# Moving rows of the big products begin 32 bytes, not 48 bytes, past a 256-byte line

## The chip, the cores and the metric

The kernel runs on one NeuronCore of one Trainium2 chip. The metric is the device time of that core in microseconds (us). The kernel before took 823.48 us (median of three runs, 822.98 to 824.05). Five engines work side by side: TensorE (PE, with its weight loads listed apart as PEld), VectorE (DVE), ScalarE (ACT), GpSimd (POOL) and SyncE (SP), which only issues transfers here. SBUF is the on-chip memory, seen as 128 partitions; an "address" below is a byte offset within each partition. Matrix products go to PSUM, read only by ACT and DVE.

## The reference

Two layers act on x, 256 tokens by 1024 features, in float32:

```
x = x + 0.5 * swiglu(rms_norm(x, ffn1_norm), ffn1_wi, ffn1_wo)         # wi 1024 x 2816, wo 1408 x 1024
u = rms_norm(x, mix_norm);  c = u @ w_in + b_in                        # w_in 1024 x 6312
y_sb  = stick-breaking attention      (4 heads of 64)
y_ml  = mLSTM, chunks of 128          (4 heads of 128)
y_mla = latent attention with rotary  (4 heads)
g = sigmoid(c.gates)                                                   # three times 1024
x = x + (g0 * (y_sb @ w_up_sb) + g1 * (y_ml @ w_up_ml) + g2 * (y_mla @ w_up_mla)) @ w_out
x = x + 0.5 * swiglu(rms_norm(x, ffn2_norm), ffn2_wi, ffn2_wo)
```

Nearly all of the arithmetic is in the products with `ffn*_wi`, `ffn*_wo`, `w_in`, `w_up_*` and `w_out`: these are the "big products".

## The kernel before, in words

**Three matmuls for one.** Both factors of a big product are split into a high and a low part of type fp32r (`hi`, `lo`), and `mm3` (L604) makes hi·hi, hi·lo and lo·hi, three matmuls that add into one PSUM tile. A matmul has a stationary operand (128 x 128, brought in by its own weight load) and a moving operand whose columns stream past it. In almost all of the big products the weights are stationary and the activations move: 256 columns, one for each token, so each partition reads a contiguous row of 256 x 4 = 1024 bytes. These are `feat_units` (L727: `ffn*_wi` and most of `w_in`), `plan_down` (L800: `ffn*_wo`, `w_out`) and `up_units` (L1086). In a smaller class the activations are stationary and the weights move, in rows of 512, 424 or 256 columns: `tok_units` (L712), the first columns of `w_in` (`first_emit`, L952) and the very last product (`plan_last`, L829).

**Where the weights lie.** SP loads a tile of weights into `raw` (`dma_tile`, L357), ACT casts it to the high part, DVE subtracts to get the low part (`conv_hi`, L364, and `conv_lo`). The two parts go into a ring of five `whi` and five `wlo` tiles, or, in the FFNs and a few other places, into two of eight tiles `g4_0` to `g4_7`. The attention outputs, which are the moving operand of `up_units`, lie in `g4` tiles as well.

**Where the moving rows lie.** `moving` (L250) makes the tiles for the activations: `u` (the normalised x) and `R1` to `R4` (the FFN's hidden activations, and the merged branches). It allocates SHIFT elements more than needed and returns the part behind them. `conv_hi` does the same inside `whi` and `wlo`, when the weights are going to be the moving operand (`w.moves`).

**What sets the addresses.** `Trunk.__init__` allocates all these tags first, in the order of `LAYOUT`. FIRST (16512) is the address at which the first one would begin; ahead of each tag a pad is put in, so that it begins at a multiple of LINE = 256 bytes. The tags' sizes are rounded up to 32 bytes, and a `whi` or `wlo` is 4352 = 17 x 256 bytes, a `g4` 4096 bytes. So every stationary weight tile begins at residue 0 of 256 bytes, and its columns are taken at steps of 512 bytes. A moving row begins at SHIFT x 4 = 48 bytes past such a multiple: rows follow each other at 1024 bytes, so all of them do. There are two exceptions: in `up_units` the moving rows lie in `g4` at residue 0, and so does a moving weight tile that was put into `g4` instead of the ring.

**What sets the order.** One Python program emits all instructions, in an order that it plans by itself: `Flow` (L79) keeps an estimated clock for each engine and for each tile the estimated time at which its pieces are ready; `drive` (L416) goes through the units of the products in order, and slips in conversions (`feed`, L377) and side work where the estimates allow it. The estimates know shapes, types and engines. Addresses come in at one place: `pieces` (L109) divides a tile into pieces of 256 bytes, counted from the tile's own beginning.

Of the kernel before, what the change touches and what calls it, by code (L numbers as in the profile page):

```python
# [202 lines left out]
class Trunk:  # L203
# [2 lines left out]
    SLACK, NEAR, BACK = 0.1, 6, 1.5  # L206


    FIRST, LINE, SHIFT = 16512, 256, 12
    LAYOUT = (("u", 4112, 1), ("R2", 2064, 1), ("R1", 2072, 1), ("R3", 784, 1), ("R4", 784, 1),  # L210
              ("whi", 1088, 5), ("wlo", 1088, 5), *((f"g4_{i}", 1024, 1) for i in range(8)))

# [1316 lines left out]
```

## Time and profile before

| | |
|---|---|
| median of three runs | 823.48 us (822.98 to 824.05) |
| profiled execution, its own time | 823.87 us |
| its span, from the first to the last instruction | 822.1 us |
| PE busy | 814.6 us, 6475 matmuls |
| DVE, ACT, POOL busy | 587.1, 455.4, 35.4 us |
| granted TensorE clock | 1.00 in the mean, the whole span |

A profile shows one execution. Matmuls overlap in the pipeline, so the busy time of one (281 ns or so) is not what it costs: the cost is its pitch, the time from one start to the next, which is read from a run of matmuls that the views put together ("x24" with the run's length). In the names, `mm<-u,whi` is a matmul into a PSUM tile `mm` with moving operand `u` and stationary operand `whi`; numbers of buffers are left out, so `R` is R1 to R4 and `g` is any `g4`.

### The profile page before, as it was taken

How to read it: one execution, taken by the hardware profiler on the slowest of the kernel's cores; microseconds unless marked ns; L12 is line 12 of the kernel's file. 1: busy time of each engine (PE TensorE's matmuls, PEld its weight loads, DVE VectorE, ACT ScalarE, POOL GpSimd, SP SyncE). 2: the span in 40 equal slices, each digit the busy share in tenths (PEclk: the TensorE clock that was granted, in tenths of full speed). 3: DMA queues.
4: the chain of work that ended last, by engine and by line, in shares of the span. 5: the costliest groups of instructions: out<-in, count | busy, mean ns of one | idle time of the engine just before them, and what ended most of it. 6: DMA issues, size and time to landing. Idle time of an engine off the chain costs nothing.

```text
span 822.1 us, 16189 instructions
## 1 busy us (share of the span) xinstructions
PE 814.6 (99%) x6475; PEld 788.0 (96%) x6475; DVE 587.1 (71%) x943; ACT 455.4 (55%) x724; POOL 35.4 (4%) x51
## 2 busy tenths in 40 slices
PE   8999999999999999999999999999999999999998
PEld 6999999899999999999999999998999999999996
DVE  5687878989667488755776567789967585886641
ACT  7456645658675546544554444665576845555430
POOL 0000000200200000000000000110003000000000
PEclk9999999999999999999999999999999999999999
DMA  8678834654264757865576554366543665587611
GB/s 257 197 226 253 266 110 137 202 156 122 85 205 153 233 167 219 258 191 168 155 228 204 179 166 141 105 207 182 157 119 112 200 183 183 179 250 218 185 67 52
DMA packets 122384, 145.41 MB, mean 177 GB/s; under 512 B 7542, under 2 KB 97092, under 8 KB 122308
## 3 DMA queue, kind: packets, MB, share of 16 engines
q1 hardware_dynamic: 122148, 144.30, 57.7%
q8 instruction: 51, 0.84, 0.4%
q14 instruction: 25, 0.20, 0.1%
q10 hardware_dynamic: 160, 0.07, 0.1%
HBM read 143.29 MB, written 1.05 MB: 176 GB/s over the span
## 4 chain that ended last, share of the span: by engine, by line
PE 94%; DMA 2%; ACT 1%; SPq 1%; DVE 1%; issue 0%; POOL 0%; DVEq 0%; ACTq 0%; POOLq 0%
PE mm L189 61%; PE at L189 33%; DMA raw<-in_ffn_wi_dram 2%; SPq L189 1%; ACT g L189 1%; DVE g L189 0%; POOL rstd L189 0%; ACT s2k L189 0%; ACT x L189 0%; ACT whi L189 0%; ACT t L189 0%; DVE s2k L189 0%; ACT u L189 0%; DVE xn L189 0%; DVE t L189 0%
## 5 line engine op out<-in xcount | busy, mean ns | idle before, releaser
L189 PE MATMUL mm<-u,whi 128*128 128x256 f32 x1728 | 312.7, 283 | 0.0
L189 ACT CAST whi<-raw 128x1024 fp32r<-128x1024 f32 (+3 forms) x186 | 190.6, 1032 | 153.9 <-PE mm L189 46.0
L189 PEld LDWEIGHTS mm<-u,whi 128*128 128x128 f32 x1728 | 264.9, 188 | 0.9 <-issue 0.7
L189 DVE TENSOR_TENSOR wlo<-raw,whi 128x1024 fp32r<-128x1024 f32 (+3 forms) x186 | 220.2, 1197 | 57.4 <-ACT whi L189 54.0
L189 PE MATMUL mm<-u,wlo 128*128 128x256 f32 x864 | 242.7, 281 | 0.0
L189 PEld LDWEIGHTS mm<-u,wlo 128*128 128x128 f32 x864 | 162.4, 188 | 0.0
L189 ACT CAST g<-raw 128x1024 fp32r<-128x1024 f32 (+3 forms) x86 | 87.3, 1021 | 79.0 <-PE mm L189 19.7
L189 PE MATMUL mm<-u,g 128*128 128x256 f32 x1056 | 129.3, 281 | 0.7 <-DVE g L189 0.7
L189 PEld LDWEIGHTS mm<-u,g 128*128 128x128 f32 x1056 | 126.6, 188 | 0.9 <-DVE g L189 0.9
L189 DVE TENSOR_TENSOR g<-raw,g 128x1024 fp32r<-128x1024 f32 (+3 forms) x86 | 101.3, 1187 | 28.0 <-ACT g L189 27.5
L189 PE MATMUL at<-R,g 128*128 128x256 f32 x594 | 72.6, 281 | 0.0
L189 PEld LDWEIGHTS at<-R,g 128*128 128x128 f32 x594 | 71.3, 188 | 0.0
L189 PE MATMUL at<-R,whi 128*128 128x256 f32 x388 | 69.5, 281 | 0.0
L189 PEld LDWEIGHTS at<-R,whi 128*128 128x128 f32 x388 | 59.4, 188 | 0.0
L189 PE MATMUL mm<-whi,u 128*128 128x512 f32 (+1 forms) x168 | 56.2, 386 | 0.0
L189 PE MATMUL at<-R,wlo 128*128 128x256 f32 x194 | 54.5, 281 | 0.0
L189 DVE TENSOR_TENSOR R<-s2k,R 128x512 fp32r<-128x512 f32 (+1 forms) x24 | 15.6, 649 | 29.4 <-ACT R L189 29.3
L189 PEld LDWEIGHTS mm<-whi,u 128*128 128x128 f32 x168 | 31.5, 188 | 5.2
L189 PEld LDWEIGHTS at<-R,wlo 128*128 128x128 f32 x194 | 36.5, 188 | 0.0
L189 PE MATMUL mm<-wlo,u 128*128 128x512 f32 (+1 forms) x84 | 32.1, 382 | 0.0
L189 POOL TENSOR_TENSOR rcol<-rcol,mhalf 128x2 f32<-128x2 f32 x6 | 7.0, 1175 | 491.6 <-DVE rcol L189 491.6
L189 ACT ACTIVATE u<-x,cols 128x256 fp32r<-128x256 f32 x40 | 18.2, 501 | 12.6 <-DVE x L189 12.6
(221 smaller groups left out, 995.8 us busy)
## 6 DMA issues: line engine op xcount, KB each, us to landing
raw<-in_w_in_dram SPq DMA_DIRECT2D x92, 512.0 KB
raw<-in_ffn_wi_dram SPq DMA_DIRECT2D x174, 256.0 KB
raw<-in_ffn_wo_dram SPq DMA_DIRECT2D x35, 512.0 KB
raw<-in_w_out_dram SPq DMA_DIRECT2D x16, 512.0 KB
raw<-in_ffn_wo_dram SPq DMA_DIRECT2D x12, 384.0 KB
raw<-in_w_up_ml_dram SPq DMA_DIRECT2D x16, 256.0 KB
raw<-in_w_in_dram SPq DMA_DIRECT2D x8, 424.0 KB
raw<-in_w_up_sb_dram SPq DMA_DIRECT2D x8, 256.0 KB
```

What stands on the lines that cost most here:

```text
L189: f(*args, **kw)
```

## The change

One constant is changed. SHIFT goes from 12 to 8 elements of 4 bytes, and with it the beginning of each moving row made by `moving`, and of the moving weights in the ring, from 48 to 32 bytes past a multiple of 256. The tags of `LAYOUT` keep their beginnings and sizes.

```
-    FIRST, LINE, SHIFT = 16512, 256, 12
+    FIRST, LINE, SHIFT = 16512, 256, 8
     LAYOUT = (("u", 4112, 1), ("R2", 2064, 1), ("R1", 2072, 1), ("R3", 784, 1), ("R4", 784, 1),
               ("whi", 1088, 5), ("wlo", 1088, 5), *((f"g4_{i}", 1024, 1) for i in range(8)))
```

## Rows read from the trace of the kernel before

**Rows 1.** The page: busy shares of PE and granted clock in 40 slices.
```profile
PE   8999999999999999999999999999999999999998
PEclk9999999999999999999999999999999999999999
```

**Rows 2.** Chain that ended last, 42.4 us to end: by line, longest pieces (start, us, what).
```profile
by line: PE mm L189 63.8%; PE at L189 34.7%; POOL rstd L189 0.3%; ACT g L189 0.2%; DVE g L189 0.2%; ACT whi L189 0.1%; issue 0.1%; ACT t L189 0.1%; DVE xn L189 0.1%; DVE t L189 0.0%; ACT R L189 0.0%
...
68.08 36.92 PE at L189 x312
...
376.18 36.92 PE at L189 x312
471.16 36.92 PE at L189 x312
```

**Rows 3.** Chain of waits, 0 to 45 us.
```profile
24.34 4.33 DMA raw<-in_ffn_wi_dram
...
35.34 4.68 DMA raw<-in_ffn_wi_dram
...
41.21 1.24 DVE g L189
```

**Rows 4.** Windows: length, busy us of PE, PEld, DVE, ACT, clock, DMA share, GB/s.
```profile
42.40:822.10 779.70, 775.33 (x6178) 752.61 (x6178) 560.57 (x887) 430.92 (x685) 34.17 (x44) 1.00 0.57 174
68.08:105.00 36.92, 36.92 (x313) 36.92 (x313) 30.05 (x38) 21.94 (x31) 0.00 (x0) 1.00 0.83 253
251.60:260.30 8.70, 8.70 (x75) 8.70 (x74) 6.84 (x9) 5.93 (x7) 0.00 (x0) 1.00 0.32 105
```

**Rows 5.** Chain of waits, 45 to 330 us, longest pieces.
```profile
147.44 16.57 PE mm L189 x72
...
251.68 2.88 PE mm L189 x24
254.56 2.88 PE at L189 x24
257.44 2.88 PE mm L189 x24
...
261.76 22.72 PE mm L189 x192
```

**Rows 6.** Groups of PE by form, 42.4 us to end: name, shapes, count, busy us, mean ns.
```profile
L189 PE MATMUL mm<-u,whi 128*128 128x256 f32 x1712 | 309.8, 283 | 0.0
L189 PE MATMUL mm<-u,wlo 128*128 128x256 f32 x856 | 240.4, 281 | 0.0
L189 PE MATMUL mm<-u,g 128*128 128x256 f32 x814 | 99.4, 281 | 0.7 <-DVE g L189 0.7
L189 PE MATMUL at<-R,g 128*128 128x256 f32 x594 | 72.6, 281 | 0.0
L189 PE MATMUL at<-R,whi 128*128 128x256 f32 x388 | 69.5, 281 | 0.0
L189 PE MATMUL at<-R,wlo 128*128 128x256 f32 x194 | 54.5, 281 | 0.0
L189 PE MATMUL mm<-whi,u 128*128 128x512 f32 x128 | 42.1, 397 | 0.0
L189 PE MATMUL mm<-wlo,u 128*128 128x512 f32 x64 | 25.1, 392 | 0.0
...
L189 PE MATMUL at<-u,g 128*128 128x256 f32 x144 | 17.7, 281 | 0.0
...
L189 PE MATMUL at<-u,whi 128*128 128x256 f32 x32 | 5.8, 281 | 0.0
...
L189 PE MATMUL at<-u,wlo 128*128 128x256 f32 x16 | 4.5, 281 | 0.0
```

**Rows 7.** Instructions that touch tile whi: duration ns min/median/max, first and last start.
```profile
L189 PEld LDWEIGHTS at<-R,whi x388: 187/188/192, 76.3 to 710.7; 128*128 128x128 f32 x194
...
L189 ACT CAST whi<-raw x186: 621/1049/1138, 28.7 to 790.7; 128x1024 fp32r<-128x1024 f32 x170, 128x768 fp32r<-128x768 f32 x9, 128x848 fp32r<-128x848 f32 x5, 128x512 fp32r<-128x512 f32 x2
L189 DVE TENSOR_TENSOR wlo<-raw,whi x186: 684/1219/1227, 29.8 to 792.4; 128x1024 fp32r<-128x1024 f32 x170, 128x768 fp32r<-128x768 f32 x9, 128x848 fp32r<-128x848 f32 x5, 128x512 fp32r<-128x512 f32 x2
...
L189 PEld LDWEIGHTS mm<-g,whi x128: 192/192/192, 251.4 to 697.9; 128*128 128x128 f32 x128
L189 PE MATMUL mm<-g,whi x128: 283/283/283, 251.5 to 698.0; 128*128 128x256 f32 x128
```

**Rows 8.** Timeline of PE in the last product: start us, us, what.
```profile
805.44 2.96 PE L189 MATMUL mm<-g,R 128*128 128x512 f32 x12
808.24 0.40 PE L189 MATMUL mm<-whi,R 128*128 128x512 f32 x1
```

## The prediction

> **What bounds the kernel now.** I read the page's slices first, then the chain of waits, then the windows. The slices show PE at nine tenths from beginning to end at full granted clock [rows 1]. The chain shows what kind of busy this is: from 42.4 us on, matmuls make up 63.8% + 34.7% = 98.5% of the chain that ended last, in pieces of 312 matmuls without one wait of another engine between them [rows 2]. Ahead of that the kernel waits for its first weights: transfers of 4.33 and 4.68 us and the conversion behind them stand in the chain, up to 42.4 us [rows 3]. Over the remaining 779.70 us DVE is busy for 560.57 and ACT for 430.92 us [rows 4]: both have slack. So the length of the kernel is, from 42.4 us on, the number of matmuls times their pitch, and a change of the pitch goes into the time nearly undiminished, in either direction.
>
> The next view is the pitch itself. With a moving row at residue 48 and weights at residue 0, 312 matmuls of 256 columns take 36.92 us: 118.33 ns each [rows 2]. A later run gives 22.72 us / 192 = 118.33 ns [rows 5]. The figure doesn't depend on the tile: one run reads `R` and the other `u`. In `up_units`, where the moving rows lie in `g4` at residue 0, the same shape takes 2.88 us / 24 = 120.0 ns, three runs one after the other with the same result [rows 5]. The weight loads tell the same: 188 ns in the median for the 48-byte rows, and 192 ns in every one of 128 loads for the 0-byte rows [rows 7]. Transfers aren't what makes the difference: DMA is busy 0.83 of the time in the run at 118.33 ns and 0.32 of it around the runs at 120.0 ns [rows 4], the wrong way round. Nor is it the clock, which is 1.00 in both [rows 4]. What remains is where the moving rows lie, and their residue is the plainest difference; that `g4` lies elsewhere in SBUF is another, which these rows can't exclude.
>
> **The change part by part.**
>
> *Instructions.* None is added or removed, no transfer, no wait. The order should stay too. The planner sees SHIFT only through the 256-byte pieces of a tile, and piece numbers come out alike: row k covers elements 256k + 12 to 256k + 267 before and 256k + 8 to 256k + 263 after, which are pieces 4k to 4k + 4 in both cases. The 128-token halves (12 to 139, now 8 to 135: pieces 0 to 2) and the moving weights (512 columns: 12 to 523, now 8 to 519: pieces 0 to 8) don't change either. So the whole effect is in what addresses do to the same instructions.
>
> *Writes by ACT and DVE.* They now write the shifted tiles at 32. The casts into `whi` take 1049 ns in the median and 1138 at most, the subtractions 1219 and at most 1227 ns, and both groups hold tiles at 0 and at 48 together [rows 7]: the residue moves them by less than 9%. Both engines have over 200 us of slack [rows 4], which hides that; if the cover were gone, 9% of the ACT casts that touch `whi`, 186 x 1.05 us, would be 18 us over the whole kernel, spread thin. I take nothing.
>
> *Moving rows of 256 columns over weights at residue 0.* Their number after 42.4 us is 1712 + 856 + 814 into `mm` from `u`, 594 + 388 + 194 from `R`, and 144 + 32 + 16 into `at` from `u`: 4750 [rows 6]. No row shows a moving row at 32, so the pitch is bounded from its neighbours. Slow side: 120.0 ns, the 0-byte rows [rows 5]. Fast side: half the pitch of a 512-column matmul with rows at 48, 16.57 us / 72 / 2 = 115.1 ns [rows 5], which would mean that a matmul had no cost of its own beside its columns. In time: +1.67 ns x 4750 = +7.9 us and -3.3 ns x 4750 = -15.5 us. A pitch above 120.0 isn't excluded either: the weight load in the open would be 188 ns, but no row comes near that.
>
> I take 120.0 ns. The reason is in the two residues known. Going from 0 to 48 changes two things, the distance, and that 48 isn't a multiple of 32 where 0 is. 32 shares the second property with 0. If SBUF is read in units of some size, a unit of 16 bytes or less would make 48 equal to 0 as well, which the two pitches deny; a unit of 32 would make 32 equal to 0; a larger one leaves it anywhere between or beyond. The smallest unit that the pitches allow is the one I take. With PE 98.5% of the chain, 0.985 x 7.9 = 7.8 us reach the end.
>
> *Moving weights.* Rows of 512 columns at 48, over stationary `u` at 48, take 16.57 us / 72 = 230.1 ns [rows 5]. Rows of 512 at 0 over stationary `R` at 48 take from 805.44 to 808.24 us for 12, 233.3 ns [rows 8]. If 32 behaves as 0, the 128 + 64 of the first kind [rows 6] lose 3.2 ns each, 0.6 us; the stationary rows move to 32 along with them, which no row prices, so I keep 0 to 0.6 us on either side and take 0.6. The few others of this class (424 and 256 columns) I leave at nothing.
>
> *Sum.* 7.8 + 0.6 = 8.4 us. The profiled execution took 823.87 us, 0.39 over the median of 823.48, so this is 832.3 in its terms and 831.9 us against the median. What is late next: nothing new. PE stays the bound, and the other engines gain slack.
>
> [...] The trace shows 118.33 ns against 120.0 ns for two residues that are both multiples of 16 [rows 2, 5]. [...]
>
> **The rivals.**
>
> *Half-way.* Gain grows with the distance from the line, or with the part of a larger unit cut off. 32 would then keep part of it: with half, 0.5 x 8.4 = 4.2 us, 827.7. For it: nothing in the trace favours 32 bytes as the unit. Against: with only two residues seen, nothing shows a slope.
>
> *Any shift will do.* The loss at 0 comes from the moving row and the weights beginning at the same residue, or from something in `g4` other than the residue. 32 then does what 48 does: 0 us, 823.5. For it: in `up_units` both begin at 0. The mechanism is that both readers start in step. Against: `tok_units` has both at 48, and 512 columns there are faster, 230.1 ns, than with the rows apart, 233.3 ns [rows 5, 8]. [...] This rival also covers a change that doesn't do what it says: if the row's place doesn't matter, the edit is without effect.
>
> *Faster.* What counts is the distance to the nearest boundary of some larger unit; were it 64 bytes, which no row shows, 48 would be 16 away and 32 the full 32. If 16 bytes bring 1.67 ns, 32 bring as much again: 116.7 ns, -1.67 x 4750 x 0.985 = -7.8 us, 815.7. It decides from the point where the pitch falls under 118.0 ns (0.2% is 1.65 us, and 1.65 us / 4750 = 0.35 ns). For it: the 512-column rows at 230.1 / 2 = 115.1 ns show that 256 columns can stream in less than 118.33 ns. Against: a row of more columns spreads a fixed cost, which explains the same figure.
>
> *Slower than 0 itself.* 32 meets the weight load worse than 0 does; no row speaks for it, and the price is open above 832.
>
> **How the numbers follow.** As slow as 0 bytes: 0.47, at 831.9. Half-way: 0.19, at 827.7. Without effect: 0.16. Faster: 0.15. Above 833: 0.03. The prediction is 831.9. A measurement can tell about 0.2%, 1.65 us, from no change. Slower is 0.47 + 0.19 + 0.03 = 0.69, the same 0.16, faster 0.15. The range from 822.5 to 833.0 holds the first three cases and leaves out 0.18, the faster one and the one above; around the likeliest alone it is 830.5 to 833.
>
> **What would show it.** In the profile of the changed kernel, the same pieces of the chain: 312 matmuls from `R` in 37.44 us (120.0 ns) instead of 36.92, and 192 from `u` in 23.04 instead of 22.72. The weight loads of `at<-R,whi` should stand at 192 ns in the median. `up_units` must keep 24 in 2.88 us; if it doesn't, residues of other tiles have moved too. 512-column pairs should come to 233 ns. The counts per group must be unchanged, or the order was changed after all. The prediction is wrong if those 312 take 36.9 us or less, and wrong in its size if they take 37.1 to 37.3.

## The result, and the profile after

The changed kernel takes 817.86 us (median of four runs, 817.43 to 818.48) against 823.39 us for the kernel before, measured beside it (four runs): a ratio of 0.9933, with a 95% interval of 0.9915 to 0.995. It is faster by 5.5 us where 8.4 us slower was forecast. The profiled execution has a span of 815.8 us, 6.3 us under that of before.

The instructions are the same on every engine and in the same order: each engine's list agrees with that of before, so that step holds. The first view is again the chain of waits from 42.4 us on, its longest pieces (start, us, what), of the changed kernel:

```profile
67.49 36.75 PE at L189 x312
...
325.90 47.60 PE mm L189 x408
373.50 36.40 PE at L189 x312
...
467.33 36.40 PE at L189 x312
```

They answer to [rows 2]: three times 312 matmuls, 264 of them from `R` and nearly all others from `u`, which took 36.92 us each before, 118.33 ns. Below, such a piece is called an `R` piece. Now one piece has 36.75 / 312 = 117.8 ns and two have 36.40 / 312 = 116.67 ns. The 408 from `u` have 47.60 / 408 = 116.67 ns. Counts and tiles are the same, the pieces are shorter. Note that one and the same kind of piece, with the same residues, has two values in one run; before, it had one.

The same chain between 45 and 330 us has the pieces that answer to [rows 5]:

```profile
146.42 16.35 PE mm L189 x72
...
249.95 2.88 PE mm L189 x24
252.83 2.88 PE at L189 x24
255.71 2.88 PE mm L189 x24
...
260.03 22.62 PE mm L189 x192
```

`up_units`, which the change doesn't touch, keeps 2.88 us / 24 = 120.0 ns: it is the control inside the run. (It has 384 matmuls in all, 128 + 64 into `mm` and as many into `at`.) The moving weights of 512 columns went from 230.1 to 16.35 / 72 = 227.1 ns. The 192 over weights at 0 went from 118.33 to 117.8 ns.

The weight loads and the casts (duration ns min/median/max), to be held against [rows 7]:

```profile
L189 PEld LDWEIGHTS at<-R,whi x388: 187/188/192, 75.7 to 705.4; 128*128 128x128 f32 x194
...
L189 ACT CAST whi<-raw x186: 621/1049/1133, 29.1 to 784.4; 128x1024 fp32r<-128x1024 f32 x170, 128x768 fp32r<-128x768 f32 x9, 128x848 fp32r<-128x848 f32 x5, 128x512 fp32r<-128x512 f32 x2
...
L189 PEld LDWEIGHTS mm<-g,whi x128: 192/192/192, 249.7 to 692.6; 128*128 128x128 f32 x128
```

The loads under the changed rows stay at 188 ns in the median, and the casts, tiles at 0 and at 32 together, at 1049 and at most 1133 ns: no cost to ACT of writing at 32 shows.

Does the pitch carry the whole difference? The `R` pieces gained 0.17 + 0.52 + 0.52 = 1.21 us over 936 matmuls, 1.3 ns each; 192 from `u` gained 0.10 us, 0.5 ns each; the 408 from `u` had 48.28 us before and have 47.60 now, 1.7 ns each. In the chain of before:

```profile
327.90 48.28 PE mm L189 x408
```

Added up from start to next start, changes of product and short waits included, the 4750 of [rows 6] took 566.6 us before and 561.3 after, 5.3 us or 1.1 ns each; the 192 wide ones took 0.4 us less. That is 5.7 us of the 6.3 by which the span went down. The first of these matmuls also starts 0.9 us earlier (41.6 against 42.5 us; 42.1 to 43.3 us in the kernels below that keep its order), which is start-up and not pitch, and what is left took 0.3 us more. So the pitch of the matmuls with a shifted row carries most of the difference between these two executions, and about as much as the medians differ by, 5.5 us.

What remained open was why 32 gives a shorter pitch than 48, when 0 gives a longer one.

### The profile page after: what moved, and what is told of

Same layout as the page of the kernel before. It is cut to its first block, busy times and chain, and to the rows that moved or that the text cites. A ratio compares the mean times of both kernels' runs of the same rounds, so it can differ in the third digit from the quotient of the medians.

```text
span 815.8 us, 16189 instructions
## 1 busy us (share of the span) xinstructions
PE 809.6 (99%) x6475; PEld 783.1 (96%) x6475; DVE 586.6 (72%) x943; ACT 455.2 (56%) x724; POOL 35.4 (4%) x51
## 4 chain that ended last, share of the span: by engine, by line
PE 92%; DMA 3%; ACT 2%; DVE 1%; SPq 1%; issue 0%; POOL 0%; ACTq 0%; DVEq 0%
PE mm L189 59%; PE at L189 33%; DMA raw<-in_ffn_wi_dram 2%; ACT g L189 1%; DVE g L189 1%; SPq L189 1%; DMA mg<-in_ml_out_norm_dram 1%; DMA R<-in_x_dram 1%; POOL rstd L189 0%; DVE qk L189 0%; ACT x L189 0%; ACT whi L189 0%; DVE wlo L189 0%; ACT s2k L189 0%; ACT R L189 0%
## 5 line engine op out<-in xcount | busy, mean ns | idle before, releaser
L189 PE MATMUL mm<-u,whi 128*128 128x256 f32 x1728 | 309.6, 281 | 0.0
```

Source lines behind the costliest of these rows:

```text
L189: f(*args, **kw)
```

## The experiments

The theories tested are: a unit of 64 (or 32) bytes, in which only the place of the moving row counts; the pair of both residues, moving row and weights; or the tile's region in SBUF, or other engines, and not the residue at all. All runs have a kernel before of their own on their chip (824.2 to 824.7 us), so ratios are compared.

**The pitch by itself.** A kernel without the network runs the same matmuls over tiles that it places at chosen residues:

```
for s in STAY:                 # 0, 16, 32, 48
    for m in MOVE:             # 0, 8, 16, 24, 32, 40, 48, 56, 64, 96, 128, 192
        run(m, s, 256, 32)     # 32 x matmul(acc, lhsT=stay[s], rhs=move[m]), 4 blocks of each in turn
```

> Leaves out the whole network: only matmuls of the network's form (fp32r, 128 x 128 stationary, a weight load for each), 32 in a row for each pair of a moving residue (0 to 192) and a stationary residue (0, 16, 32, 48), 256 columns, no other engine at work; then 16 in a row of 512 columns. Pitch by theory. Unit of 64 bytes, what counts is where the moving row begins in it: 0, 64, 128 and 192 alike at 120.0 ns, 32 lowest near 117, 16 and 48 near 118.3, 96 like 32, and the stationary residue changes little. Distance from the weights: each pitch depends only on the difference of the two residues, so 0 over 0, 16 over 16 and 32 over 32 are all 120.0, and 0 over 32 is like 32 over 0. Other engines or the region of g4 and not the residue: every pair of one column count within 0.3 ns.

The timeline of PE (start us, us, what; letters stand for residues: `mva` is 0, `mvb` 8, `mvc` 16, `mvd` 24, `mve` 32, `mvf` 40, `mvg` 48, `mvh` 56; `sta` is 0):

```profile
31.18 3.99 PE L50 MATMUL acc<-mva,sta 128*128 128x256 f32 x32
35.01 4.00 PE L50 MATMUL acc<-mvb,sta 128*128 128x256 f32 x32
38.85 3.90 PE L50 MATMUL acc<-mvc,sta 128*128 128x256 f32 x32
42.59 4.00 PE L50 MATMUL acc<-mvd,sta 128*128 128x256 f32 x32
46.42 3.90 PE L50 MATMUL acc<-mve,sta 128*128 128x256 f32 x32
50.16 4.00 PE L50 MATMUL acc<-mvf,sta 128*128 128x256 f32 x32
54.00 3.95 PE L50 MATMUL acc<-mvg,sta 128*128 128x256 f32 x32
57.79 4.00 PE L50 MATMUL acc<-mvh,sta 128*128 128x256 f32 x32
```

The distance from one run's start to the next run's, divided by 32, is the pitch with its change-over: 0 over 0 has 3.83 us / 32 = 119.7 ns, 32 over 0 has 3.74 / 32 = 116.9, and 48 over 0 has 3.79 / 32 = 118.4. Without the first matmuls of each run they are 119.8, 116.7 and 118.4. These are the kernel's own figures (120.0, 116.67 to 117.8, 118.33) with no other engine at work and no weights being brought in. Two things follow: the places of the two operands are enough to make these pitches, and neither ACT and DVE, nor a stream of weights, nor the region of `g4` are needed for them. The unit of 64 bytes fell as well: 64 over 0 has 117.8 ns and 192 over 0, after some first steps of 118 to 124 ns, 113.3 (the 113.7 below has some of those in it), where it wants 119.8 for both. So did the difference of the residues alone: 48 over 48 has 118.2, and 0 over 0 119.8.

**Other shifts in the kernel.** Four runs change the one constant, or the place of the `g4` tiles:

```
-    FIRST, LINE, SHIFT = 16512, 256, 8
+    FIRST, LINE, SHIFT = 16512, 256, 4       # 16 bytes; in three more: 16 (64 bytes), 0, 48 (192 bytes)
```

> SHIFT 4, moving rows at 16 bytes. Unit of 64 bytes with its best point in the middle: 16 mirrors 48, 312 matmuls of R in 36.9 us and the time near 823. More cut off the better, up to 32 only: between 0 and 32, near 823 too. Distance from the weights with no mirror: anything, but 16 must differ from 64. Any shift that isn't 48: like the changed kernel, 818.

> SHIFT 16, moving rows at 64 bytes. Unit of 64 bytes: same as 0, 120.0 ns for 256 columns, 4750 x 1.67 ns x 0.985 = 7.8 us over the kernel before, 831. Unit of 128 or 256 bytes: 64 keeps a gain, 818 to 824.

> SHIFT 0, moving rows and weights both at residue 0. The isolated pitch table gives 119.8 ns for 0 over 0 against 118.4 for 48 over 0 and 116.7 for 32 over 0. If that table carries over to the kernel: 4750 x (119.9 - 118.33) ns x 0.985 = 7.3 us over the kernel before, about 1%, and so 32 and 0 are opposite ends and not one class. If the table doesn't carry over, because in the kernel other engines use SBUF too: anything else, and 120.0 ns in up_units is due to its tiles.

> SHIFT 48, moving rows at 192 bytes, tags of u and R1 to R4 made 32 elements longer (all still begin at residue 0). The isolated table has 113.7 ns for 192 over 0, the lowest of all. If it carries over: 4750 x (118.33 - 113.7) ns x 0.985 = 21.7 us under the kernel before, 802. Unit of 64 bytes: as 0, 831. Some chance order of matmuls and loads and not the residue made the 113.7: near 64, 816.

| moving rows at | ratio to before | 95% interval | the three `R` pieces |
|---|---|---|---|
| 0 | 1.0055 | 1.0038 to 1.0071 | 37.44, 37.44, 37.44 us |
| 16 | 0.997 | 0.9956 to 0.9983 | 35.36, 37.02, 36.40 us |
| 48 (before) | 1 | | 36.92, 36.92, 36.92 us |
| 32 (the change) | 0.9933 | 0.9915 to 0.995 | 36.75, 36.40, 36.40 us |
| 64 | 0.9899 | 0.9885 to 0.9914 | 36.74, 35.36, 36.74 us |
| 192 | 0.9803 | 0.9781 to 0.9825 | 36.75, 35.36, 36.75 us |

The pieces are those of one execution each; the one of 16 was the fastest of its seven (818.27 us, the median is 821.07). The chains of 0 and of 192:

```profile
69.34 37.44 PE at L189 x312
...
380.12 37.44 PE at L189 x312
...
476.35 37.44 PE at L189 x312
```

```profile
67.95 36.75 PE at L189 x312
...
370.64 35.36 PE at L189 x312
...
463.04 36.75 PE at L189 x312
```

With 0 the pitch is 37.44 us / 312 = 120.0 ns, against 119.8 alone; the time rose by 0.55% instead of the 0.9% expected. SHIFT 0 changes the planner's pieces and so the order (1680 matmuls `mm<-u,whi` in place of 1728 in the whole kernel), so its time isn't only the pitch. 32 and 0 are thus far from one class: they lie on either side of 48. With 64 and 192 the forecasts of the unit theories fail. 16 fits none of its forecasts well: its time is a little under that of 48. With 192 the place is the second best found, but at 808.67 us it is 16 us under the kernel before and not the 21.7 expected, since its pitch isn't steady: 35.36 us / 312 is 113.33 ns, the isolated figure, and 36.75 us is 117.8 ns, in one run.

**The weights moved under the rows.** The changed kernel with all `g4` tiles 32 bytes further (a small constant tile goes into a pad to make room):

```
-            pad = -end % self.LINE
+            pad = (32 * (tag == "g4_0") - end) % self.LINE if tag[:3] != "g4_" or tag == "g4_0" else 0
```

> The changed kernel with all g4 tiles 32 bytes further, so that up_units' moving rows begin at 32 over weights at 0, and the FFN weights that lie in g4 are stationary at 32 under moving rows at 32. Residue of the moving row: up_units falls from 120.0 to about 117.2 ns, 640 x 2.8 ns = 1.8 us less, the FFN stays, 816. Region of g4: up_units stays at 120.0, 818. Distance from the weights: up_units falls, but the some 1,500 FFN matmuls over g4 weights rise to 120.0, about 4.4 us more, 820 to 821.

Ratio 0.995 (0.9935 to 0.9965), 820.28 us. Its chain:

```profile
69.15 36.91 PE at L189 x312
...
251.63 2.80 PE mm L189 x24
...
261.43 22.40 PE mm L189 x192
```

`up_units`, now 32 over 0, fell from 2.88 to 2.80 us: 116.7 ns. It was the residue and not the region. (The forecast's "640" should be 384 matmuls, 1.3 us; from start to start they took 1.25 us less.) At the same time the `R` piece, which mixes `g4` weights (now 32 over 32) with ring weights (32 over 0), rose from 36.75 and 36.40 to 36.91 us, while 192 matmuls over the ring alone stand at 22.40 / 192 = 116.67 ns. The moving rows of that `R` piece weren't touched; only the weights beneath them were. Added up from start to start, the 1552 with a moving row over `g4` went from 117.3 ns in the mean to 120.0, 4.3 us more, as the distance theory had it, and the 3198 over the ring from 118.6 to 118.1. Over the three groups that makes 1.5 us more than in the changed kernel, 0.17% as between the ratios 0.9933 and 0.995. Moving row alone is thus out: the weights' place counts as well.

**The whole table.** All pairs of 16 moving and 16 stationary residues, and narrower stationary operands:

> Leaves out the whole network: pitch of the network's matmuls (fp32r, 256 columns, a weight load each), 28 in a row, for moving residues 0 to 240 and stationary residues 0 to 240 in steps of 16, then moving residues 256 to 496 over 0, then 64 and 32 stationary columns instead of 128 over moving 0 to 240. Conflict of two readers in banks of a 256-byte period: 256 + r repeats r; the pitch hangs on the pair; with 64 and 32 stationary columns the residue matters less and the pitch goes to one floor, since there is less of a second reader. Moving row alone: the residue matters as much with 32 stationary columns as with 128.

The timeline of PE (`mvag` is moving 96, `mvah` 112, `mvba` 128, `mvch` 368; `staa` is 0; 128*64 and 128*32 have 64 and 32 stationary columns):

```profile
75.42 3.51 PE L51 MATMUL acc<-mvag,staa 128*128 128x256 f32 x28
78.77 3.36 PE L51 MATMUL acc<-mvah,staa 128*128 128x256 f32 x28
81.97 3.48 PE L51 MATMUL acc<-mvba,staa 128*128 128x256 f32 x28
...
927.25 3.36 PE L51 MATMUL acc<-mvch,staa 128*128 128x256 f32 x28
...
956.93 3.34 PE L51 MATMUL acc<-mvaa,staa 128*64 128x256 f32 x28
960.11 3.43 PE L51 MATMUL acc<-mvab,staa 128*64 128x256 f32 x28
...
1009.18 3.34 PE L51 MATMUL acc<-mvaa,staa 128*32 128x256 f32 x28
1012.36 3.36 PE L51 MATMUL acc<-mvab,staa 128*32 128x256 f32 x28
```

Here the length of a run of 28 tells the pitch: 27 pitches and the last matmul's 0.28 us or so. 3.36 us is 113.3 to 114.3 ns, 3.51 us some 119.5 to 120; the first few steps can differ from the rest. From the starts of the sixth to the last matmul of each run, in ns, by the difference of the residues (moving less stationary, modulo 256), the median of eight pairs each:

```
difference                  0    16    32    48    64    80    96   112   128   144   160   176   192   208   224   240
weights at  0, 32, 64 .. 119.7 118.7 116.5 118.4 117.8 120.0 119.9 113.3 118.4 118.9 117.3 119.2 117.8 119.3 118.3 117.2
weights at 16, 48, 80 .. 118.2 117.5 118.2 116.7 118.3 118.2 120.0 120.0 120.0 120.1 116.7 118.7 113.3 123.3 119.9 118.3
```

Moving both residues on by 32 leaves the pitch within 0.3 ns in 244 of the 256 pairs, moving both by 16 in only 18. So in this run the pitch follows the difference of the two residues modulo 256, with a second table for weights that begin at an odd multiple of 16. In the first row stand the two kernels: difference 48, 118.4 ns, and 32, 116.5 ns. Ending the period at 256 is right too: the sixteen moving residues from 256 to 496 repeat those from 0 to 240 within 0.1 ns, as 368 = 256 + 112 repeats the 113.3 ns of 112.

The pair isn't the whole of it. Of the 32 pairs that stand in both isolated runs, seven differ by more than 0.3 ns: 16 over 0 has 116.7 ns in the first and 118.7 in the second, 192 over 0 113.3 and 117.8. In the second run each pair comes just after the one with its moving residue 16 lower, so this order repeats along with the differences; it is broken at the sixteen pairs with moving 0, and five of these stand off their column, by 0.5 to 5.0 ns (0 over 64: 113.3 against 117.8), against three of the other 240. The tiles of the two runs also begin at other multiples of 256. So the places of both operands matter, but one pair can have more than one pitch.

With 64 stationary columns 0 over 0 falls from 119.9 to 113.3 ns, but 240 over 0 still has 120.0; with 32 columns ten of the sixteen moving residues stand within 0.4 ns of 113.3, against one of sixteen with 128, and the highest is 117.7. This fits the weight load as the other reader, and so do the two runs that move weights under rows left in place: 117.3 to 120.0 ns with `g4` at 32, and 113.3 to some 118 with the ring at 80 (below). A narrower stationary operand also gives an output of fewer rows, though, and no run tells these apart. What the two reads do to each other inside SBUF no run shows.

**The lowest pair in the kernel, and a test in one run.** 112 over 0 is the lowest, and its column holds 113.3 to 113.4 ns in all eight pairs:

```
-    FIRST, LINE, SHIFT = 16512, 256, 8
+    FIRST, LINE, SHIFT = 16512, 256, 28      # sizes of u and R1 to R4 up by 8 to 16 elements, beginnings as before
-            o = self.SHIFT if w.moves else 0
+            o = self.SHIFT if w.moves else 20    # second kernel only: ring weights at 80
```

> SHIFT 28, moving rows at 112 bytes, the isolated table's steady low: 113.3 ns over 0, and alike at 368. Conflict of moving reads and weight reads, set by both residues modulo 256: 4750 x (118.33 - 113.33) ns x 0.985 = 23.4 us under the kernel before, ratio 0.972, with 312 matmuls of R in 35.4 us. If the kernel blurs the table as it did at 32 (117.1 against 116.5): 0.6 ns and 2.8 us less than that. Unit of 32 or 64 bytes: 112 is in the class of 48, ratio 1.00.

> Moving rows at 112, stationary weights in the ring moved to 80, those in g4 left at 0. Pair of residues decides: in one and the same run, matmuls of u or R over g4 weights keep 113.3 ns, those over ring weights go to 118.2 (112 over 80 in the table), and up_units, 0 over 80, falls from 120.0 to 118.8. Moving row alone decides: over g4 and over the ring alike, 113.3, up_units at 120.0. Time about 3,000 x 4.9 ns = 15 us over the run with the ring at 0.

112 alone gives 803.09 us, a ratio of 0.9745 (0.9732 to 0.9759), between the full forecast, 23.4 us, and the one with a blur. The chain of that run:

```profile
67.34 35.36 PE at L189 x312
...
247.20 2.88 PE mm L189 x24
...
367.59 35.36 PE at L189 x312
458.87 35.36 PE at L189 x312
```

35.36 us / 312 is 113.33 ns, three times out of three: this pair is steady in the kernel too, and not blurred. From start to start all 4750 took 21.3 us less than in the kernel before, 4.5 ns each and not 5.0: changes of product and short waits are in that sum. The time fell by 21.1 us. With the ring at 80 besides, its one execution took 817.51 us, 14.4 us more. In that run the busy times of the matmuls from `R` (min/median/max) part by where the weights lie:

```profile
L189 PE MATMUL at<-R,g x594: 275/275/283, 72.5 to 716.8; 128*128 128x256 f32 x198
...
L189 PE MATMUL at<-R,whi x388: 276/280/285, 75.3 to 705.7; 128*128 128x256 f32 x194
```

Over `g4` at 0 they have 275 ns, over the ring at 80 they have 280. A busy time isn't a pitch, but the timeline of PE has that as well:

```profile
72.55 2.93 PE L189 MATMUL at<-R,g 128*128 128x256 f32 x24
75.32 0.40 PE L189 MATMUL at<-R,whi 128*128 128x256 f32 x2
75.55 0.28 PE L189 MATMUL at<-R,wlo 128*128 128x256 f32 x1
75.67 0.40 PE L189 MATMUL at<-R,whi 128*128 128x256 f32 x2
```

The 24 over `g4` start at 72.55 and the next matmul at 75.32 us, 115.4 ns each: the first nine, which come after matmuls over the ring, go at steps of 116 to 121 ns, the others at 113 or 114. The ring's triples follow at 75.32, 75.67 and 76.03, some 118 ns. The same tiles move in both. `up_units`, 0 over 80, fell to 2.85 us / 24 = 118.75 ns, as the table has it (118.8):

```profile
250.21 2.85 PE mm L189 x24
```

**The last product at 120 ns.** On top of 112, the ring weights of `up_units` alone are put at 224:

```
+            w0.off = w1.off = 56             # conv_hi: o = self.SHIFT if w.moves else w.off
```

> Moving rows at 112, and the ring weights of up_units alone at 224, under moving rows that lie in g4 at 0. Pair of residues: up_units falls from 120.0 to 116.7 ns (0 over 224), 640 x 3.3 ns = 2.1 us under the run with 112 alone, ratio 0.9695 to the kernel before. Region of g4 or moving row alone: up_units stays at 120.0 and the time at that of 112 alone.

```profile
248.54 2.80 PE mm L190 x24
```

`up_units` fell to 2.80 us / 24 = 116.7 ns, as forecast, but the time, 803.3 us (0.9737, 0.9722 to 0.9751), can't be told from that of 112 alone. On its 384 matmuls (the forecast took 640) 3.3 ns make 1.3 us and not 2.1, some 0.15% of the time, and the intervals of the two overlap: not shown as a gain. The profiled execution lost more than that elsewhere: between 42 and 48 us its granted clock is 0.72 in the mean (1.00 with 112 alone), and fifteen matmuls there follow each other at 213 ns; the first 214 matmuls of the chain from 42 us on take 26.21 us, against 24.54 with 112 alone. Of its five executions the two with a mean granted clock of 1.0 took 801.0 and 801.8 us, the three such ones with 112 alone 803.1 each; that agrees with 1.3 us, but two are too few to show it.

## Why the prediction was wrong

- *What bounds the kernel* held. PE's pitch goes into the time nearly undiminished: 5.3 us less on the 4750 matmuls, from start to start, and 0.4 on the wide ones came out as 5.5 us, and 21.3 us less, with 112, as 21.1.
- *No instruction changes, nor their order* held, and so did *writes by ACT and DVE* at nothing.
- *The step that failed* is "I take 120.0 ns", with its reason that a unit of 32 bytes "would make 32 equal to 0" and "The smallest unit that the pitches allow is the one I take". No such unit shows: the pitch goes up and down with the difference from the weights over the whole 256 bytes, from 113.3 to 120.0 ns over weights at 0. Measured: 116.5 to 116.7 ns for 32 over 0 in the isolated runs, and 116.67 to 117.8 ns in the kernel. With two points of such a table, nothing could be read between them. The honest range for the pitch was the one that I had worked out from the rows, 115.1 to 120.0 ns, and the predicted range should have reached down with it; it stopped at 822.5 and left the faster rival out.
- *The bound of 115.1 ns* wasn't a floor either: 113.33 ns stands in the kernel at 112.
- *The weight loads* don't "tell the same". Their median is 192 ns where the pitch is 120.0 (in `up_units`, and with SHIFT 0 under `R` as well), and 188 ns at 118.33, at 116.67 and at 113.33 alike, so among these it marks off the slowest place and says nothing of the others.
- *Moving weights*: forecast 0.6 us slower; in the long pieces each of the 192 took 3 ns less, and all together, from start to start, 0.4 us less. The 233.3 ns taken for 32 came from another pair, 0 over 48. With both operands at 0 the wide rows take 16.35 us / 72 = 227.1 ns, so 0 is no slow place for them, and their 230.1 ns was no evidence against *Any shift will do* either.
- *Faster*, the rival, had the sign and nearly the size (815.7 against 817.86), but by luck: its mechanism is the distance to a boundary of 64 bytes, and 64 and 192, which lie on one, are better than 32 (ratios of 0.9899 and 0.9803 against 0.9933).
- *Any shift will do* came nearest to the cause, that the weights' place counts too: in `up_units` both begin at 0, and that costs, 120.0 ns against 116.7 with either of them moved (`g4` to 32, the weights to 224). But "apart" isn't enough: 96 over 0 has 119.9 ns and 8 over 0 120.0.
- *Two residues that are both multiples of 16*, with two pitches, were no exception: over pairs of such residues, with nothing else at work, the pitch runs from 113.3 to 123.4 ns. The place of the weights has a part in that for fp32r operands with a load for each 256 columns: by it alone 1552 matmuls went from 117.3 to 120.0 ns.

Open: why one pair can have several pitches. 64 over 0 gave 35.36 us and 36.74 us for the same 312 matmuls in one run, and 192 over 0 gave 113.3 ns in the first isolated run and 117.8 in the second. With 16, which had three pitches in one run, the seven executions also lie 6 us apart (818.27 to 824.22), with 112 four lie within 0.7 us. What went just before a piece may choose, as the broken order in the second isolated run and the nine slow steps over `g4` suggest; no run changed that alone.

## What to carry to other kernels

Where PE is busy without a gap, read the pitch from runs in the chain of waits, and not the busy time of a matmul: in this kernel 5 ns of 118, 2.5% of the time, hung on where tiles begin. Here the place of a moving row had to be set against that of the weights (by the weights' place alone 117.3 ns became 120.0), and a table of pairs, measured by a small kernel with nothing else in it, carried over to the big one within 1.3 ns for 0, 32, 48 and 112 over 0. It did not for 16, 64 and 192, which had more than one pitch in the kernel, up to 5.4 ns from an isolated figure: measure a place more than once, after different neighbours, before trusting it. Two points of this table, 120.0 ns at 0 and 118.33 at 48, said nothing of a third, 116.67 to 117.8 at 32.

## What the runs showed of the hardware that was not expected

- A pitch of 113.3 to 123.4 ns for the same matmul of 256 fp32r columns with its weight load, at a granted clock of 1.0 and with no other engine at work, by where its two operands begin modulo 256 bytes and, for some pairs, by something else that is open.
- Moving rows that begin 8, 24, 40 or 56 bytes past a multiple of 256, over weights at 0, all have 119.9 to 120.0 ns in the first isolated run.
- Wide rows prefer other places: 512 columns with both operands at 32 have 227.1 ns in the kernel, as with both at 0, at 48 230.1 and at 112 16.79 us / 72 = 233.2 ns.
